# GpSimd's two-operand instructions of 512 columns in halves of 256, in a hybrid attention and RWKV block

## The chip, the cores and the metric

The kernel runs on one core of a Trainium2 chip. The metric is the device time of one execution in microseconds (us); the number that stands for a kernel is the median of its runs. Five engines work side by side, each through its own queue in order: TensorE (PE; its weight loads are PEld), VectorE (DVE), ScalarE (ACT), GpSimd (POOL) and SyncE (SP, which only issues DMAs here).

## What is computed

One layer of a residual block on 1024 frames of width 1024. The mixer has two groups of heads: A is sparse attention in which an indexer picks the 256 best keys of each frame, B is an RWKV-7 recurrence over 64-frame chunks. An MLP of width 4096 with squared ReLU follows. Cut to what matters:

```python
mod = silu(c) @ w_ada + b_ada                       # shift, scale, gate, twice
h = rms_norm(x, g_mix) * (1 + sc1) + sh1
proj = h @ w_in                                     # columns of group A, then of group B
o_a = dsa_attention(...)                            # index scores, top 256 keys, softmax
o_b = rwkv7_time_mix(token_shift(p_b, mu), ...)     # state * w + sa kk a + v k, per head
x = x + gt1 * (concat(o_a, o_b) @ w_out)
h = rms_norm(x, g_ffn) * (1 + sc2) + sh2
u = relu(h @ w_ff1)
x = x + gt2 * ((u * u) @ w_ff2)
```

## The kernel before

The 1024 frames are worked in two halves of 512 (`HALF`), features on the partitions and frames on the columns, so nearly every tile is 128 partitions x 512 columns.

**The large products.** `dense` (L391) makes one 128 x 512 product of `w_in`, `w_out`, `w_ff1` or `w_ff2`. Each operand is held as a rounded part and its remainder, and three matmuls take the place of one: hi x hi, hi x lo, lo x hi. For four blocks of weights at a time `load_w` (L378) fetches `wraw`, ACT rounds it to `whi` (L384), and POOL, or in the last stage DVE, subtracts: `wlo = wraw - whi` (L386). `LE = 'gggggggv'` says that POOL does it in all stages but the last, the MLP of the second half. `wlo` is 128 x 4 x 128, four buffers deep; the matmuls of `dense` read it one block of 128 columns at a time, in the order block 0, 1, 2, 3:

```python
mmul(ps[0:M], hi[:, k, 0:M], rh(K), start=(K == 0), stop=False)
mmul(ps[0:M], hi[:, k, 0:M], rl(K), start=False, stop=False)
mmul(ps[0:M], lo[:, k, 0:M], rh(K), start=False, stop=(K == nk - 1))
```

**The recurrence.** `rwkv_feat` (L486) prepares a pair of heads. POOL's part is `kp` (L523), `at` (L532), the second half of `KR` (L552), `wrec` (L558) and the two halves of `BKs` (L562, L563); DVE works between, with `rk` (L537), the first half of `KR` (L550) and `Bh` (L557). PE waits for `rk` with a product of its own. `rwkv_inv` inverts the chunk matrices with a long row of small DVE instructions, `rwkv_chain` runs the chunks, and `rwkv_out` normalises, with POOL's `On` (L718) and `ob` (L724). There are eight pairs of heads in all, four in each half. Which engine does such a step is set by `EM = 'gggggggggv'` through `EN`, whose result is GpSimd for `g`.

**The indexer.** `indexer` finds the 256th best score of each frame bit by bit, 31 bits: a count over the scores (`jk`, L911 and L913, on DVE; `jka`, L905, on ACT), then a few tiny DVE instructions (L926, L927, L902; L920, L928, L903) that set the next candidate. It runs beside the projections of the second half, and again beside the first MLP.

**The order of the work** is made by a scheduler that takes the instructions as the code gives them and sets them on the engines' queues by what it takes each to cost; a change of one engine's instructions can so move others.

Of the kernel before, what the change touches and what calls it, by code (L numbers as in the profile page):

```python
# [4 lines left out]
F32 = mybir.dt.float32  # L5
# [4 lines left out]
ALU = mybir.AluOpType  # L10
# [25 lines left out]
LE = 'gggggggv'  # L36
# [7 lines left out]
NL = 'gg'  # L44
# [3 lines left out]
EM = 'gggggggggv'  # L48
# [63 lines left out]
def body(tc, I, out, dbg=None):  # L112
    nc = tc.nc
    V, G, A, T = nc.vector, nc.gpsimd, nc.scalar, nc.tensor
# [5 lines left out]
    def mmul(out, lhsT, rhs, start=True, stop=True, **kw):  # L120
        r = T.matmul(out, lhsT, rhs, start=start, stop=stop, **kw)  # L121
        MM[0] = r
        if MK[0]:
            MARKS.append((MK[0], int(r.ins.name.split("-")[1])))
            MK[0] = None
        return r

    def EN(i):
        return V if EM[i] == "v" else G

    def mark(n):
        MK[0] = n
# [10 lines left out]
    def pst(tag):  # L143
        return pm.tile([128, 512], F32, name="ps_" + tag, tag=tag, bufs=BANKS[tag])
# [11 lines left out]
    def C(name, a=0, b=None):  # L156
        o, w = CC[name]
        t = con if o < NCF else conb
        o -= 0 if o < NCF else NCF
        return t[:, o + a:o + (w if b is None else b)]  # L160

    def P(name, a=0, b=None):
        o, w = PC[name]
        return prm[:, o + a:o + (w if b is None else b)]
# [21 lines left out]
    def sigmoid(out, x, bias=0.0):  # L186

        A.activation(out, x, AF.Tanh, scale=0.5, bias=bias)
        EN(8).tensor_scalar(out, out, 1.0, 0.5, ALU.add, ALU.mult)
# [104 lines left out]
    def h_tiles(hp=hp):  # L294
        hh = hp.tile([128, 8, HALF], F32R, name="hh", tag="hh", bufs=1)
        hl = hp.tile([128, 8, HALF], F32R, name="hl", tag="hl", bufs=1)
        return hh, hl
# [25 lines left out]
    def norm_last(hf, xn, xp, nb):  # L323
        mark('norm%d' % hf)
        hh, hl = h_tiles()
        for k in range(8):
            v = xp.tile([128, HALF], F32, name="nv", tag="nv", bufs=nb)
            V.tensor_scalar(v, xn[k], g1[:, k:k + 1], mod[:, k:k + 1], ALU.mult, ALU.add)
            A.copy(hh[:, k, :], v)
            (V if NL[hf] == "v" or k % 2 == 0 else G).tensor_tensor(hl[:, k, :], v, hh[:, k, :].bitcast(F32), ALU.subtract)  # L330
        return hh, hl

    def load_xT(hf, xp):
# [44 lines left out]
    def load_w(w, row0, col0, M):  # L378

        raw = wp.tile([128, 4, 128], F32, name="wraw", tag="wraw", bufs=WB[0])  # L380
        nc.sync.dma_start(raw[:, :, 0:M], w[row0:row0 + 512, col0:col0 + M].rearrange("(k p) n -> p k n", p=128))
        hi = wp.tile([128, 4, 128], F32R, name="whi", tag="whi", bufs=WB[1])
        lo = wp.tile([128, 4, 128], F32R, name="wlo", tag="wlo", bufs=WB[1])
        (A.copy if HE[GRP[0]] == "a" else V.tensor_copy)(hi[:, :, 0:M], raw[:, :, 0:M])  # L384
        GRP[1] ^= 1
        (V if LE[GRP[0]] == "v" or LE[GRP[0]] == "m" and GRP[1] else G).tensor_tensor(lo[:, :, 0:M], raw[:, :, 0:M], hi[:, :, 0:M].bitcast(F32), ALU.subtract)  # L386
        return hi, lo

    GRP = [0, 0]
# [63 lines left out]
    def spread(dst, i, j, sl):  # L453
        for h in range(2):
            nc.sync.dma_start(dst[h * 64:h * 64 + 64], rnd[i][2 * j + h:2 * j + h + 1, sl].to_broadcast([64, HALF]))
# [26 lines left out]
    def c3(x):  # L482
        return x.rearrange("p (c t) -> p c t", t=64)
# [4 lines left out]
    def rwkv_feat(hf, j, L4, rp, bp):  # L488

        mark('feat%d%d' % (hf, j))  # L490
        tw, xa, sg = L4
        sl = slice(hf * HALF, hf * HALF + HALF)

        def tmp(nm, tag=None, bufs=1):
            return rp.tile([128, HALF], F32, name=nm, tag=tag or nm, bufs=bufs)

        rT, kT = tmp("rT"), tmp("kT")
        v2 = rp.tile([128, 8, 64], F32, name="v2", tag="v2", bufs=1)
        nc.sync.dma_start(kT, rkvd[4 + j, :, sl])
        nc.sync.dma_start(rT, rkvd[j, :, sl])  # L500
        nc.sync.dma_start(v2, c3(rkvd[8 + j, :, sl]))
        gp = bp if j % 2 else rp
        KR, Lb = (gp.tile([128, 8, 2, 64], F32, name=n, tag=n, bufs=1) for n in ("KR", "Lb"))
        WC = gp.tile([128, 8], F32, name="WC", tag="WC", bufs=1)
        bvs = (bp if j % 3 else rp).tile([128, HALF], F32, name="bvs", tag=f"bvs{j % 3}", bufs=1)

        sig = rp.tile([128, 4, 128], F32, name="sig", tag="wincl", bufs=1)
        ps = pst("f")
        for tt in range(4):
            mmul(ps[:, tt * 128:tt * 128 + 128], tw[:, tt * 128:tt * 128 + 128], w2a[:, j * 128:j * 128 + 128])  # L510
        sigmoid(sig, ps.rearrange("p (a b) -> p a b", a=4))
        prn = tmp("prn", "aT")
        spread(prn, 0, j, sl)
        kap = tmp("kap")
        V.scalar_tensor_tensor(kap, kT, P("k_k", j, j + 1), prn, ALU.mult, ALU.mult)
        pa = pst("f")
        mmul(pa, a2w[:, j * 128:j * 128 + 128], xa)

        at = tmp("at", "aT")
        A.activation(at, pa, AF.Tanh, scale=0.5, bias=a0h[:, j:j + 1])  # L520
        kp = tmp("kp")
        A.activation(kp, at, AF.Identity, scale=kah[:, j:j + 1], bias=oka[:, j:j + 1])
        EN(0).tensor_tensor(kp, kp, kT, ALU.mult)  # L523
        b2 = at
        if FO == -1:
            G.tensor_scalar(at, at, 1.0, 0.5, ALU.add, ALU.mult)
            G.tensor_tensor(b2, kap, at, ALU.mult)
        elif FO == 0:
            V.scalar_tensor_tensor(b2, at, 1.0, kap, ALU.add, ALU.mult)
        elif FO == 1:  # L530
            A.activation(b2, at, AF.Identity, bias=1.0)
            G.tensor_tensor(b2, b2, kap, ALU.mult)  # L532
        else:
            G.tensor_scalar(b2, at, 1.0, 1.0, ALU.add, ALU.mult)
            G.tensor_tensor(b2, b2, kap, ALU.mult)
        rk = tmp("rk", "Bh")
        V.scalar_tensor_tensor(rk, rT, P("r_k", j, j + 1), kp, ALU.mult, ALU.mult)  # L537
        pb = pst("f")
        slow[hf, j] = mmul(pb, C("oblk"), rk)
        V.tensor_tensor(c3(bvs), c3(pb), v2, ALU.mult)  # L540
        pw = pst("f")
        for tt in range(4):
            mmul(pw[:, tt * 128:tt * 128 + 128], sig[:, tt, :], C("tri"))
        wi, wr = tmp("wincl"), tmp("wrec", bufs=2)
        A.activation(wi, pw, AF.Exp, scale=-EM05)
        A.activation(wr, pw, AF.Exp, scale=EM05)
        wi3 = c3(wi)
        V.tensor_copy(WC, wi3[:, :, 63])

        V.tensor_tensor(KR[:, :, 0, 1:64], c3(kap)[:, :, 1:64], wi3[:, :, 0:63], ALU.mult)  # L550
        V.tensor_copy(KR[:, :, 0, 0], c3(kap)[:, :, 0])
        EN(2).tensor_tensor(KR[:, :, 1, :], c3(rT), wi3, ALU.mult)  # L552
        Bh, Kh = tmp("Bh"), wr
        if FO == -1:
            V.tensor_tensor(Bh, b2, wr, ALU.mult)
        else:
            V.scalar_tensor_tensor(Bh, b2, 0.5, wr, ALU.mult, ALU.mult)  # L557
        EN(3).tensor_tensor(Kh, kp, wr, ALU.mult)  # L558
        gram(Bh, KR, Lb, "f")
        BKs = rp.tile([128, 8, 2, 64], F32, name="BKs", tag="BKs", bufs=1)  # L560
        wcb = WC.unsqueeze(2).to_broadcast([128, 8, 64])
        EN(4).tensor_tensor(BKs[:, :, 0, :], c3(Bh), wcb, ALU.mult)  # L562
        EN(5).tensor_tensor(BKs[:, :, 1, :], c3(Kh), wcb, ALU.mult)  # L563
        return dict(KR=KR, Lb=Lb, WC=WC, bvs=bvs, Kh=Kh, BKs=BKs, v2=v2)

    def gram(src, KR, dst, tag):
        for u in (0, 4):
            pz = pst(tag)
            for c in range(4):
                cc = u + c  # L570
                for h in range(2):
                    r = slice(h * 64, h * 64 + 64)
                    mmul(pz[r, c * 128:c * 128 + 128], src[r, cc * 64:cc * 64 + 64], flat(KR[r, cc, :, :]),
                         tile_position=(h * 64, h * 64))
            V.tensor_tensor(dst[:, u:u + 4, :, :].rearrange("p a b c -> p a (b c)"),
                            pz.rearrange("p (a b) -> p a b", a=4),
                            C("zmask").unsqueeze(1).to_broadcast([128, 4, 128]), ALU.mult)
# [738 lines left out]
```

## Time and profile before

| what | value |
|---|---|
| runs, median (lowest to highest of 3) | 1803.91 us (1803.64 to 1807.76) |
| profiled execution, its own time | 1806.86 us |
| its span, first to last instruction | 1805.0 us |
| PE busy | 1621.7 us, 90% |
| DVE busy | 1084.3 us, 60% |
| ACT busy | 870.9 us, 48% |
| POOL busy | 484.8 us, 27%, 423 instructions |
| mean granted clock of TensorE | 0.968 |

The profile is of one execution. An engine's busy share is a mean over the span; PE's matmuls overlap, so its busy time is no measure of how full it is. POOL has no work in the last 375 us: its last `wlo` starts at 1429.1 us. An instruction's time in the trace reaches from its start to its end and holds what it waited for after its start.

### The profile page before, as it was taken

What the parts mean: (1) busy time and instruction counts of PE and PEld (TensorE: products, weight loads), DVE (VectorE), ACT (ScalarE), POOL (GpSimd) and SP (SyncE); (2) the same over time, 40 slices, a digit from 0 to 9 for tenths busy, and PEclk for the clock granted to TensorE, in tenths of its full rate; (3) what the DMA queues carried; (4) which work ended last, traced back from release to release, by engine and by line L of the source; (5) the groups of instructions that cost most, each with busy time, mean ns of one, the idle gap of its engine ahead of it and who ended that gap; (6) DMA issues with size and microseconds to landing.
All of it is one profiled execution on the core that took longest, in us unless ns stands there. A gap on an engine that the chain in (4) does not pass through costs nothing. (4 is left out here: it accounts for less than half of the span.)

```text
span 1805.0 us, 26789 instructions
## 1 busy us (share of the span) xinstructions
PE 1621.7 (90%) x9380; PEld 1210.2 (67%) x9380; DVE 1084.3 (60%) x2701; ACT 870.9 (48%) x1792; POOL 484.8 (27%) x423
## 2 busy tenths in 40 slices
PE   6896888998779887998968888999999999999998
PEld 3674655666555565665647666777886788888887
DVE  4787677649987666846999648773213333333333
ACT  3323454545546544544855773775335252525251
POOL 2445333343340133332123343012444300000000
PEclk9998999999989999999978999999999999999999
DMA  9785225334343452212112234233432343333332
GB/s 309 248 298 181 84 69 176 110 91 135 99 113 104 151 159 83 80 51 70 48 41 70 70 94 129 79 86 116 124 95 75 100 128 94 99 94 98 96 94 75
DMA packets 264013, 203.86 MB, mean 113 GB/s; under 512 B 17300, under 2 KB 218004, under 8 KB 263879
## 3 DMA queue, kind: packets, MB, share of 16 engines
q1 hardware_dynamic: 253122, 182.90, 34.1%
q10 hardware_dynamic: 10628, 19.24, 2.8%
q8 instruction: 74, 1.21, 0.3%
q14 instruction: 61, 0.49, 0.1%
q0 software_dynamic: 128, 0.01, 0.0%
HBM read 173.32 MB, written 28.78 MB: 112 GB/s over the span
## 5 line engine op out<-in xcount | busy, mean ns | idle before, releaser
L386 POOL TENSOR_TENSOR wlo<-wraw,whi 128x512 fp32r<-128x512 f32 x256 | 345.1, 1352 | 741.4 <-ACT whi L384 632.0
L384 ACT CAST whi<-wraw 128x512 fp32r<-128x512 f32 x384 | 235.8, 617 | 418.4 <-PE ps_mm L121 384.9
L121 PE MATMUL ps_mm<-hh,whi 128*128 128x512 f32 (+1 forms) x1024 | 415.3, 407 | 20.8 <-DVE shy L428 6.7
L121 PE MATMUL ps_mm<-hh,wlo 128*128 128x512 f32 (+1 forms) x1024 | 415.5, 406 | 5.3 <-POOL wlo L386 5.1
L121 PE MATMUL ps_mm<-hl,whi 128*128 128x512 f32 (+1 forms) x1024 | 416.1, 407 | 3.5 <-DVE hl L374 2.0
L121 PEld LDWEIGHTS ps_mm<-hh,whi 128*128 128x128 f32 (+1 forms) x1024 | 194.2, 190 | 68.4 <-DVE shy L428 8.4
L121 PEld LDWEIGHTS ps_mm<-hh,wlo 128*128 128x128 f32 (+1 forms) x1024 | 194.4, 190 | 50.3 <-POOL wlo L386 10.0
L121 PEld LDWEIGHTS ps_mm<-hl,whi 128*128 128x128 f32 (+1 forms) x1024 | 194.6, 190 | 45.9 <-issue 5.1
L121 PE MATMUL ps_mm<-uh,whi 128*128 128x512 f32 x512 | 206.9, 405 | 18.7 <-ACT whi L384 5.4
L121 PE MATMUL ps_mm<-ul,whi 128*128 128x512 f32 x512 | 206.6, 404 | 5.8 <-DVE ul L1108 5.8
L121 PE MATMUL ps_mm<-uh,wlo 128*128 128x512 f32 x512 | 206.3, 403 | 2.0 <-POOL wlo L386 1.9
L386 DVE TENSOR_TENSOR wlo<-wraw,whi 128x512 fp32r<-128x512 f32 x128 | 88.3, 690 | 130.1 <-ACT whi L384 130.1
L905 ACT ACTIVATE jka<-sc,canda 128x1024 bf16<-128x1024 f32 (+1 forms) x93 | 90.2, 970 | 86.8 <-DVE canda L903 59.4
L121 PEld LDWEIGHTS ps_mm<-uh,whi 128*128 128x128 f32 x512 | 98.9, 193 | 46.1 <-ACT whi L384 9.4
L121 PEld LDWEIGHTS ps_mm<-ul,whi 128*128 128x128 f32 x512 | 98.7, 193 | 29.9 <-DVE ul L1108 8.0
L121 PEld LDWEIGHTS ps_mm<-uh,wlo 128*128 128x128 f32 x512 | 98.9, 193 | 26.6 <-POOL wlo L386 4.0
L1114 DVE SCALAR_TENSOR_TENSOR xT<-ps_mm,mod,xT 128x512 f32<-128x512 f32 x64 | 47.9, 749 | 111.6 <-PE ps_mm L121 111.5
L1108 DVE TENSOR_TENSOR ul<-ur,uh 128x512 fp32r<-128x512 f32 x64 | 44.2, 691 | 80.0 <-ACT uh L1107 80.0
L1013 DVE CUSTOM_DVE_ANT_0 L<-ps_f,mk 128x512 f32<-128x512 f32 (+3 forms) x96 | 51.8, 554 | 34.3 <-PE ps_f L121 16.9
L695 ACT COPY Ub<-ps_c 64x64 f32<-64x64 f32 x128 | 26.3, 206 | 74.1 <-DVE UV L693 65.3
L1019 ACT ACTIVATE L<-L,m 128x128 f32<-128x128 f32 (+7 forms) x64 | 49.6, 775 | 18.6 <-DVE m L1016 13.8
L1032 ACT COPY PT<-ps_c 128x512 f32<-128x512 f32 (+3 forms) x96 | 42.6, 479 | 31.0 <-PE ps_c L1031 29.3
(329 smaller groups left out, 2623.1 us busy)
## 6 DMA issues: line engine op xcount, KB each, us to landing
wraw<-in_w_ff_dram SPq DMA_DIRECT2D x256, 256.0 KB
wraw<-in_w_in_dram SPq DMA_DIRECT2D x92, 256.0 KB
mraw<-in_w_ada_dram SPq DMA_DIRECT2D x64, 256.0 KB
mraw<-in_w_ada_dram SPq DMA_DIRECT2D x16, 512.0 KB
wraw<-in_w_out_dram SPq DMA_DIRECT2D x32, 256.0 KB
rkvd<-shy ACTq DMA_DIRECT2D x24, 256.0 KB
xin<-in_x_dram SPq DMA_DIRECT2D x8, 512.0 KB
rt<-rnd SPq DMA_DIRECT2D x32, 128.0 KB
```

What stands on the lines that cost most here:

```text
L121: r = T.matmul(out, lhsT, rhs, start=start, stop=stop, **kw)
L384: (A.copy if HE[GRP[0]] == "a" else V.tensor_copy)(hi[:, :, 0:M], raw[:, :, 0:M])
L386: (V if LE[GRP[0]] == "v" or LE[GRP[0]] == "m" and GRP[1] else G).tensor_tensor(lo[:, :, 0:M], raw[:, :, 0:M], hi[:, :, 0:M].bitcast(F32), ...
L695: (V.tensor_copy if CE[2] == "v" else A.copy)(Ub[h * 64:h * 64 + 64, h, :], pu[u, h * 64:h * 64 + 64])
L905: A.activation(jka[:, 0:width(b)], sc[b], AF.Sign, scale=-1.0, bias=0.0 if bit == 31 else canda.bitcast(F32)[:, i:i + 1], accum_out=ca[:, ...
L1013: V.tensor_tensor_reduce(L[:, c0:c0 + n], ps[:, 0:n], masks[b][:, c0:c0 + n], 1.0, -3e38, ALU.add, ALU.max, m2[:, pc:pc + 1])
L1019: A.activation(L[:, 0:W], L[:, 0:W], AF.Exp, bias=m2[:, 2:3], accum_out=m2[:, 3:4])
L1032: (A.copy if ((pc + h) % 2 if PTE == 0 else h if PTE == 1 else PTE == 2) else V.tensor_copy)(pT[:, c0:c0 + n], px[:, 0:n])
L1108: V.tensor_tensor(b, r, a.bitcast(F32), ALU.subtract)
L1114: V.scalar_tensor_tensor(xT[:, d, :], ps, mod[:, 40 + d:41 + d], xT[:, d, :], ALU.mult, ALU.add)
```

## The change

A class `InHalves` stands where `G` (GpSimd) stood: in `EN`, in `norm_last`, in `load_w` and in `rwkv_feat`. Its `tensor_tensor` issues two instructions, one on the first half of the second axis and one on the other; its `tensor_scalar` is GpSimd's as it was. The second axis of `wlo` has four blocks of 128 columns, so a half is two blocks; of the others it has 512 columns or 8 chunks. The narrow `wlo` of 4 x 72 columns is cut to 2 x 72 as well. Nothing else is changed: what is computed, which engine does it, buffers and DMAs are the same. Split are 256 `wlo`, 8 `hl`, and eight each of `kp`, `at`, `KR`, `wrec`, `On`, `ob` and the two `BKs`: 328 instructions become 656.

```diff
+    class InHalves:
+
+        tensor_scalar = G.tensor_scalar
+
+        @staticmethod
+        def tensor_tensor(o, a, b, op):
+            n = o.shape[1] // 2
+            for c in (slice(0, n), slice(n, 2 * n)):
+                G.tensor_tensor(o[:, c], a[:, c], b[:, c], op)
+
     def EN(i):
-        return V if EM[i] == "v" else G
+        return V if EM[i] == "v" else InHalves
...
-            (V if NL[hf] == "v" or k % 2 == 0 else G).tensor_tensor(hl[:, k, :], v, hh[:, k, :].bitcast(F32), ALU.subtract)
+            (V if NL[hf] == "v" or k % 2 == 0 else InHalves).tensor_tensor(hl[:, k, :], v, hh[:, k, :].bitcast(F32), ALU.subtract)
...
-        (V if LE[GRP[0]] == "v" or LE[GRP[0]] == "m" and GRP[1] else G).tensor_tensor(lo[:, :, 0:M], raw[:, :, 0:M], hi[:, :, 0:M].bitcast(F32), ALU.subtract)
+        (V if LE[GRP[0]] == "v" or LE[GRP[0]] == "m" and GRP[1] else InHalves).tensor_tensor(lo[:, :, 0:M], raw[:, :, 0:M], hi[:, :, 0:M].bitcast(F32), ALU.subtract)
...
-            G.tensor_tensor(b2, b2, kap, ALU.mult)
+            InHalves.tensor_tensor(b2, b2, kap, ALU.mult)
```

The order of the instructions shows it at three places. The first is POOL's queue at the first pair of heads (`rwkv_feat`); before:

```order
L523 TENSOR_TENSOR kp<-kp,kT 128x512
L532 TENSOR_TENSOR at<-at,kap 128x512
L386 TENSOR_TENSOR wlo<-wraw,whi 128x512 x3
L552 TENSOR_TENSOR KR<-rT,wincl 128x8x64
L558 TENSOR_TENSOR wrec<-kp,wrec 128x512
```

and now, where every split instruction is at L136:

```order
L136 TENSOR_TENSOR kp<-kp,kT 128x256 x2
L136 TENSOR_TENSOR at<-at,kap 128x256 x2
L136 TENSOR_TENSOR wlo<-wraw,whi 128x256 x6
L136 TENSOR_TENSOR KR<-rT,wincl 128x4x64 x2
L136 TENSOR_TENSOR wrec<-kp,wrec 128x256 x2
```

The steps stand in the same order, each as two.

The second is PE's queue in the projections of the first half, with what a matmul waits for; `wlo` is the weights' remainder and Pool_49 POOL's semaphore. Before:

```order
L121 MATMUL ps_mm<-hh,wlo 128x512 [waits Pool_49]
L121 MATMUL ps_mm<-hh,whi 128x512
L121 MATMUL ps_mm<-hl,whi 128x512
L121 MATMUL ps_mm<-hh,wlo 128x512
L121 MATMUL ps_mm<-hh,whi 128x512
L121 MATMUL ps_mm<-hl,whi 128x512
L121 MATMUL ps_mm<-hh,wlo 128x512
```

and now:

```order
L121 MATMUL ps_mm<-hh,wlo 128x512 [waits Pool_49]
L121 MATMUL ps_mm<-hh,whi 128x512
L121 MATMUL ps_mm<-hl,whi 128x512
L121 MATMUL ps_mm<-hh,wlo 128x512
L121 MATMUL ps_mm<-hh,whi 128x512
L121 MATMUL ps_mm<-hl,whi 128x512
L121 MATMUL ps_mm<-hh,wlo 128x512 [waits Pool_49]
```

The first matmul with `wlo` waits for the first half alone, and the one on block 2, six matmuls later, for the second.

The third is ACT's queue where the first search of the indexer begins (`rl` are index scores, `jka` its counts on ACT); before:

```order
L867 ACTIVATE rl<-ps_f 128x384
L867 ACTIVATE rl<-ps_f 128x512
L384 CAST whi<-wraw 128x512
L905 ACTIVATE jka,ca<-sc_3837 128x512
L419 DMA rkvd<-shy 128x512
L384 CAST whi<-wraw 128x512
L905 ACTIVATE jka,ca<-sc_3837,canda 128x512
```

and now:

```order
L394 CAST whi<-wraw 128x512
L877 ACTIVATE rl<-ps_f 128x384
L877 ACTIVATE rl<-ps_f 128x512
L429 DMA rkvd<-shy 128x512
L915 ACTIVATE jka,ca<-sc_3925 128x512
L394 CAST whi<-wraw 128x512
L915 ACTIVATE jka,ca<-sc_3925,canda 128x512
```

One rounding of weights stands two score tiles earlier, and a DMA ahead of the first count instead of behind it. Such shifts lie between PE's rows 988 and 2203 of some 6050, from the last pair of heads of the first half to the start of the second indexer (in the trace of before, from 400 to some 845 us); ahead of them and behind them PE's order is the same.

## Rows read from the trace of the kernel before

**Rows 1.** Busy time by stretch: PE, PEld, DVE, ACT, POOL, granted clock, DMA share, GB/s.
```profile
0.00:1100.00 1100.00, 931.98 (x5951) 660.48 (x5952) 797.79 (x2161) 561.17 (x1252) 378.06 (x341) 0.95 0.39 121
1100.00:1805.00 705.00, 689.73 (x3431) 549.75 (x3429) 286.56 (x541) 309.75 (x540) 106.74 (x82) 1.00 0.34 100
...
900.00:1000.00 100.00, 81.05 (x293) 60.12 (x294) 96.57 (x270) 51.69 (x95) 31.01 (x22) 0.83 0.19 56
```

**Rows 2.** POOL's groups by shape (busy us, mean ns, idle before); last, L386's minimum/median/maximum.
```profile
L386 POOL TENSOR_TENSOR wlo<-wraw,whi 128x512 fp32r<-128x512 f32 x252 | 341.9, 1360 | 726.8 <-ACT whi L384 624.4 <-PE ps_mm L121 39.7 <-DMA kr<-khd 16.0
L386 POOL TENSOR_TENSOR wlo<-wraw,whi 128x288 fp32r<-128x288 f32 x4 | 3.2, 801 | 14.6 <-ACT whi L384 7.6 <-ACT On L703 4.5 <-DMA prn<-rnd 2.5
...
L386 POOL TENSOR_TENSOR wlo<-wraw,whi x256: 791/1289/2042, 39.6 to 1429.1; 128x512 fp32r<-128x512 f32 x126, 128x288 fp32r<-128x288 f32 x2
```

**Rows 3.** Timeline of DVE, then POOL, at 150 us (start, us, instruction).
```profile
150.44 1.64 DVE L281 SCALAR_TENSOR_TENSOR macc<-mraw,cs,macc 128x512 f32<-128x512 f32 x1
152.00 1.75 DVE L537 SCALAR_TENSOR_TENSOR rk<-rT,prm,kp 128x512 f32<-128x512 f32 x1
...
150.26 1.28 POOL L523 TENSOR_TENSOR kp<-kp,kT 128x512 f32<-128x512 f32 x1 [4.20 <-ACT kp L522]
151.50 1.71 POOL L532 TENSOR_TENSOR at<-at,kap 128x512 f32<-128x512 f32 x1
```

**Rows 4.** Timeline of DVE, then POOL, at 930 us, in the second indexer.
```profile
930.49 1.01 DVE L911 TENSOR_SCALAR_CACHE_REDUCE jk<-top,cand 128x768 bf16<-128x768 bf16 x1
...
931.54 0.37 DVE L926 TENSOR_SCALAR acc<-cv 128x2 int32<-128x2 f32 x1
931.95 1.19 DVE L927 TENSOR_TENSOR pre<-pre,acc 128x2 int32<-128x2 int32 x1
...
930.61 2.50 POOL L386 TENSOR_TENSOR wlo<-wraw,whi 128x512 fp32r<-128x512 f32 x2 [6.25 <-ACT whi L384]
```

**Rows 5.** DVE's groups by shape (busy us, mean ns, idle before).
```profile
L926 DVE TENSOR_SCALAR acc<-cv 128x2 int32<-128x2 f32 x31 | 15.1, 488 | 0.5
L926 DVE TENSOR_SCALAR acc<-cv 128x1 int32<-128x1 f32 x31 | 4.7, 152 | 0.6
L928 DVE TENSOR_TENSOR prea<-prea,acca 128x1 int32<-128x1 int32 x31 | 14.7, 474 | 0.2
L281 DVE SCALAR_TENSOR_TENSOR macc<-mraw,cs,macc 128x512 f32<-128x512 f32 x56 | 51.7, 923 | 2.3 <-DMA mraw<-in_w_ada_dram 0.8
L1114 DVE SCALAR_TENSOR_TENSOR xT<-ps_mm,mod,xT 128x512 f32<-128x512 f32 x64 | 47.9, 749 | 111.6 <-PE ps_mm L121 111.5
L550 DVE TENSOR_TENSOR KR<-kap,wincl 128x504 f32<-128x504 f32 x8 | 11.2, 1406 | 0.1
L754 DVE TENSOR_TENSOR rt<-rt 128x512 f32<-128x512 f32 x8 | 5.5, 686 | 0.1
L537 DVE SCALAR_TENSOR_TENSOR rk<-rT,prm,kp 128x512 f32<-128x512 f32 x8 | 10.1, 1259 | 2.7 <-POOL kp L523 2.7
```

**Rows 6.** PE's waits by releaser: us in total, times, longest.
```profile
PE ps_f L121 <- DVE rk L537: 14.3, 6, 6.8
PE ps_f L121 <- DVE acca L920: 7.9, 1, 7.9
PE ps_mm L121 <- POOL wlo L386: 7.0, 11, 1.1
PE ps_mm L121 <- DVE acca L920: 6.2, 5, 1.7
PE ps_c L721 <- POOL On L718: 2.7, 2, 2.1
```

**Rows 7.** Timeline of PE, POOL and ACT at 1033 us.
```profile
1034.59 0.50 PE L121 MATMUL ps_mm<-hh,wlo 128*128 128x512 f32 x1 [0.62 <-POOL wlo L386]
...
1033.26 1.27 POOL L386 TENSOR_TENSOR wlo<-wraw,whi 128x512 fp32r<-128x512 f32 x1 [2.44 <-ACT whi L384]
...
1032.56 0.62 ACT L384 CAST whi<-wraw 128x512 fp32r<-128x512 f32 x1
```

## The prediction

> **What bounds the kernel now.** I read the busy time by stretch first. Up to 1100 us the stages are mixed: PE is busy for 932 of 1100 us, DVE for 798. Behind that PE is busy for 690 of 705 us and little can be won; POOL has work there until 1429 us, but PE hardly waits for it [rows 1]. PE's queue sets the pace throughout, and what this change can move is PE's waiting in the first 1100 us. The second indexer is the tightest place of DVE: from 900 to 1000 us it is busy for 96.6 us, PE for 81, and PE's granted clock is 0.83 there [rows 1].
>
> PE's waits by releaser come next. For POOL itself PE waits little: 7.0 us for `wlo`, 2.7 us for `On`. It waits more for DVE: 14.3 us for `rk`, 7.9 and 6.2 us put down to the indexer's counts [rows 6]. The timelines show what POOL has to do with that. At 150.44 us DVE issues a sum (`macc`) and is done only at 152.08, as POOL's `kp` ends at 151.54; then `rk` stands from 152.00 to 153.75 until POOL's `at` has ended at 153.21; and POOL's `at` itself takes 1.71 us because it stood behind the DVE sum [rows 3]. At 931.95 us a DVE instruction on two columns takes 1.19 us beside POOL's `wlo`, while the count of 768 columns just ahead of it ran its 1.01 us beside the same POOL work undisturbed [rows 4]. So POOL's two-operand instructions and part of DVE's shut each other out, one whole instruction at a time, and between two POOL instructions one waiting DVE instruction gets through: at 931.54 DVE goes after the first of POOL's pair, and the next DVE instruction waits for the second [rows 4].
>
> What that costs DVE is read from its groups, mean against the mean of the like group that meets no POOL work [rows 5]: the count's step L926 (488 - 152) x 31 = 10.4 us, L928 (474 - 152) x 31 = 10.0, `macc` (923 - 749) x 56 = 9.7, `KR` (1406 - 686) x 8 = 5.8, `rk` (1259 - 749) x 8 = 4.1: 40.0 us in five groups.
>
> **The price of a half.** No POOL row has 256 columns; the nearest is the narrow `wlo` with 288: 801 ns against 1360 for 512 [rows 2]. The line through both means gives 2.50 ns a column and 82 ns fixed, so 722 ns for a half and 1444 for the pair, 84 more than before. Through the median 1289 in place of the mean, 2.18 ns a column and 174 fixed: 732 and 1463, 174 more. I take 0.13 us a pair, with both as ends. 328 pairs make 43 us more on POOL, which is busy for 485 of 1805 us: hidden, as long as nobody waits for the second half. If the cover went, it would be the 14 pairs of the third term that pay. The Trainium skill's GPSIMD Engine Reference (section Performance versus the Vector engine) puts a two-input instruction at about 2.6 cycles an element at 1.2 GHz; an estimate from it is 555 ns for 256 columns, and with the median's remainder of 180 ns each the third term would be 2.5 us in place of 1.8. No row here shows it at 256.
>
> **The terms.**
> First, `wlo` comes earlier: its first two blocks land after 0.72 us in place of 1.29, and PE needs the other two only six matmuls later. Eleven PE waits of together 7.0 us end with it [rows 6]; 0.57 us off each would be 6.3 us at most. But six of them, 0.6 us each, lie between 1030 and 1050 us and look like the one shown, where ACT rounds `whi` with no idle time in front of it [rows 7]: PE would reach the next `whi` sooner and wait there. Of the other five I take 2 us: **-2**, between -6.3 and 0.
>
> Second, blocked DVE instructions. Where POOL's pair is `wlo`, made ahead of time, and the DVE instruction let in after the first half is the last that needs POOL's way, the second half runs beside undisturbed DVE work and half of the block is gone. Where another such DVE instruction follows at once, the second half blocks that one, and the sum stays. In the indexer three tiny ones follow each other ahead of an undisturbed count, so one in three: 20.4 x 1/3 x 1/2 = 3.4 us, and 4 with the like of the groups not shown. For `macc`, back to back, nothing; for `rk` and `KR` nothing, since there the POOL instruction is itself on the way to the same result, and two jobs behind one door take their sum in either order. **-4**, between -10 (half of all 40 us, and half of that on the path, as 28.4 us of PE's waits stand behind these chains [rows 6]) and 0.
>
> Third, POOL's results that PE waits for come later: six waits for `rk` with two split steps ahead of them (`kp`, `at`) and two for `On` [rows 6], 14 pairs x 0.13 = 1.8: **+2**. If a DVE instruction of 512 columns (0.75 us [rows 5]) slips between the halves each time, 14 x 0.75 = 10.5 us more.
>
> The added semaphore waits on PE I cost at nothing: they are for the second half, and the six matmuls ahead of it cover more than its 0.72 us. DVE and ACT get no instruction more, SP's DMAs are the same, and what stands behind a POOL instruction in POOL's queue is moved by the 0.13 us alone. The scheduler's shifts between 400 and 845 us have no row that prices them; I take 0, with 1 us on either end.
>
> The sum is -4 us. The profiled execution took 1806.9 us, 3 us above the median of the runs (1803.9); against its own time the sum gives 1802.9, against the median **1800**.
>
> **The rivals.** A change within 0.3% (5.4 us) is about what a measurement of this kernel cannot tell from none.
>
> *Faster, DVE is freed.* If most blocked DVE instructions stand alone, every block halves: term two is -10, and 1803.9 - 2 - 10 + 2 gives **1794**. For it: PE's waits behind DVE are the largest of the mixed stages [rows 6], and DVE fills the second indexer, where the clock is low too [rows 1]. Against it: at 931 us it was the very next DVE instruction that the second POOL instruction held [rows 4]. Chance 0.37.
>
> *No change, as many blocks as before.* In the runs of small DVE instructions, each half shuts out one. The second term is then 0, and the port's time grows by 0.13 us for each of some 20 blocks in L926 and L928 (20.4 us at nearly 1 us each): +3. 1803.9 - 2 + 3 + 2 = **1807**. The Trainium skill's page SBUF — State Buffer (section Who interferes with whom) has it that issue order, not the shape of the operation, decides who is blocked; by that rule a smaller shape wins nothing as such. Rows 4 bear it out as far as one DVE instruction goes through between two of POOL's. Chance 0.13. It also stands for the change not doing what it says: if POOL's second half takes the way before the waiting DVE instruction, two halves block like one whole, and the time is near 1804.
>
> *Slower, POOL's own chain is cut in two.* Each of the 14 pairs that PE waits for lets a DVE instruction in between its halves, one that used to wait until the whole was done: `macc` at 150.44 would now go in the middle of `kp`, and `rk` waits for `kp` [rows 3]. That is 10.5 us: 1803.9 - 2 + 10.5 + 2 = **1814**. It decides from some seven such pairs up (7 x 0.75 = 5.3), if the second term is nothing. Against it: the same interposed work need not be done later, so on `rk`'s way much comes back. Chance 0.22.
>
> **How the numbers follow.** The forecast of 1800 has 0.28. It and the rival near 1807 lie within 0.3%: 0.41. Faster by more, 0.37; slower by more, 0.22. The range reaches from 1803.9 - 6.3 - 10, and 1 for the order, 1786.6, rounded to 1786, to the slower rival's 1814 and 1 for the order, 1815. The outer tenth on either side is left for the scheduler's shifts and for PE's clock, whose low stretches neither bound holds.
>
> **What would show it.** Right: POOL's halves near 0.72 us and 656 of them; the six `wlo` waits at 1030 us gone and waits for `whi` in their place; L926 and L928 at means some 15% lower, with the other tiny instructions of the search a little longer; `rk` and `KR` as long as before, give or take the order. Wrong: if `rk`, `KR` and L926 all come down by half of their excess, DVE was freed; if PE's waits for `rk` and `On` grow by half a us each, the chain was cut; if the time moves between 400 and 845 us alone, it was the order.

## The result, and the profile after

The changed kernel takes **1789.09 us** (median of 5 runs, 1783.01 to 1792.60) beside 1805.34 us (5 runs, 1803.64 to 1807.97) for the kernel before: a ratio of 0.99, 95% interval 0.9876 to 0.9923. It is faster by 1%. The forecast of 1800 us, no change that can be told, was 11 us too long; the range of 1786 to 1815 holds the time, and of the rivals the one that frees DVE (1794) came nearest.

The profiled execution took 1783.31 us, at the low end of the runs, with a span of 1781.5 us (1805.0 before). The page's first part:

```profile
PE 1613.9 (91%) x9380; PEld 1208.7 (68%) x9380; DVE 1060.6 (60%) x2701; ACT 871.5 (49%) x1792; POOL 557.7 (31%) x751
```

DVE does the same 2701 instructions in 23.7 us less; POOL needs 72.9 us more. PE's busy time falls by 7.8 us and the span by 23.5, so two thirds of the gain are PE's idle time (183.3 us before, 167.6 after). The other third is PE's own work: the same 9380 matmuls, at a mean granted clock of 0.971 beside 0.968.

POOL's groups by shape (busy us, mean ns, idle before), against [rows 2]:

```profile
L136 POOL TENSOR_TENSOR wlo<-wraw,whi 128x256 fp32r<-128x256 f32 x504 | 396.5, 810 | 643.8 <-ACT whi L394 582.3 <-DMA kr<-khd 15.9 <-PE ps_mm L121 10.8
L136 POOL TENSOR_TENSOR wlo<-wraw,whi 128x144 fp32r<-128x144 f32 x8 | 4.1, 527 | 14.3 <-ACT whi L394 7.5 <-ACT On L713 4.3 <-DMA prn<-rnd 2.4
```

A half has a mean of 810 ns with what it waited for; undisturbed, a pair takes 1.44 us (below), 0.72 a half, as the prediction had it.

DVE's groups by shape, against [rows 5] (lines are 10 higher; L936, L938, L291, L560 and L547 are L926, L928, L281, L550 and L537):

```profile
L936 DVE TENSOR_SCALAR acc<-cv 128x2 int32<-128x2 f32 x31 | 10.0, 322 | 0.5
L938 DVE TENSOR_TENSOR prea<-prea,acca 128x1 int32<-128x1 int32 x31 | 7.7, 247 | 0.3
L291 DVE SCALAR_TENSOR_TENSOR macc<-mraw,cs,macc 128x512 f32<-128x512 f32 x56 | 50.3, 899 | 3.0 <-DMA mraw<-in_w_ada_dram 1.4
L560 DVE TENSOR_TENSOR KR<-kap,wincl 128x504 f32<-128x504 f32 x8 | 7.3, 918 | 0.1
L547 DVE SCALAR_TENSOR_TENSOR rk<-rT,prm,kp 128x512 f32<-128x512 f32 x8 | 8.8, 1097 | 3.0 <-POOL kp L136 3.0
L937 DVE TENSOR_TENSOR pre<-pre,acc 128x2 int32<-128x2 int32 x31 | 10.4, 335 | 0.8
```

By the working of the prediction the excess of the five groups goes from 40.0 us to (322 - 152) x 31 = 5.3, (247 - 152) x 31 = 2.9, (899 - 749) x 56 = 8.4, (918 - 686) x 8 = 1.9 and (1097 - 749) x 8 = 2.8, together 21.3: close to half. But part of that only moved. L937, the step behind L936, grew from 295 to 335 ns, and so did the step behind L938, which is L903 before and L913 now:

```profile
L903 DVE SCALAR_TENSOR_TENSOR canda<-prea,xma 128x1 int32<-128x1 int32 x31 | 7.8, 253 | 0.2
```

```profile
L913 DVE SCALAR_TENSOR_TENSOR canda<-prea,xma 128x1 int32<-128x1 int32 x31 | 9.8, 317 | 0.2
```

There a second half blocks the next instruction. All groups of the search's small steps (`acc`, `pre`, `prea`, `cand`, `canda`) went from 80.4 to 76.1 us together: of the 12.1 us that L936 and L938 lost, the steps behind them took 7.8 back. So DVE's 23.7 us are 4.3 from these steps, 6.6 from `macc`, `KR` and `rk`, and 12.8 spread over its other instructions, no group of which lost more than 2.6.

Both cases stand in the timelines. At the first pair of heads, DVE's row and then POOL's, against [rows 3]:

```profile
145.87 1.89 DVE L291 SCALAR_TENSOR_TENSOR macc<-mraw,cs,macc 128x512 f32<-128x512 f32 x2
148.38 1.19 DVE L547 SCALAR_TENSOR_TENSOR rk<-rT,prm,kp 128x512 f32<-128x512 f32 x1 [0.62 <-POOL kp L136]
...
146.46 1.88 POOL L136 TENSOR_TENSOR kp<-kp,kT 128x256 f32<-128x256 f32 x2 [2.38 <-ACT kp L532]
148.30 1.86 POOL L136 TENSOR_TENSOR at<-at,kap 128x256 f32<-128x256 f32 x2
```

`kp` takes 1.88 us in place of 1.28, because a DVE sum (the second `macc`) goes between its halves; but `rk` then stands only behind the first half of `at`, and is done 3.11 us after `kp` began (148.38 + 1.19 - 146.46) in place of 3.49. In the second indexer, against [rows 4]:

```profile
913.77 0.53 DVE L936 TENSOR_SCALAR acc<-cv 128x2 int32<-128x2 f32 x1
914.33 0.65 DVE L937 TENSOR_TENSOR pre<-pre,acc 128x2 int32<-128x2 int32 x1
915.00 0.65 DVE L912 SCALAR_TENSOR_TENSOR cand<-pre,xmh 128x2 int32<-128x2 int32 x1
915.69 0.88 DVE L921 TENSOR_SCALAR_CACHE_REDUCE jk<-top,cand 128x640 bf16<-128x640 bf16 x1
...
912.84 2.80 POOL L136 TENSOR_TENSOR wlo<-wraw,whi 128x256 fp32r<-128x256 f32 x4 [5.56 <-ACT whi L394]
```

Two `wlo` follow each other, and three tiny DVE instructions pay for three of the four halves: 1.92 us from 913.77 to the next count, about the 1.83 us of before, from 931.54 [rows 4] to this count:

```profile
933.37 0.88 DVE L911 TENSOR_SCALAR_CACHE_REDUCE jk<-top,cand 128x640 bf16<-128x640 bf16 x1
```

Here nothing was won. One DVE instruction goes through between every two of POOL's.

PE's waits by releaser, against [rows 6]:

```profile
PE ps_f L121 <- DVE rk L547: 15.7, 7, 5.3
PE ps_f L121 <- DVE acca L930: 8.4, 1, 8.4
PE ps_mm L121 <- ACT whi L394: 7.0, 7, 2.5
PE ps_c L731 <- POOL On L136: 5.7, 2, 3.5
...
PE ps_mm L121 <- DVE acca L930: 5.0, 3, 2.5
...
PE ps_mm L121 <- POOL wlo L136: 0.5, 1, 0.5
```

The waits for `wlo` are gone (7.0 to 0.5 us). All of PE's waits that a DVE instruction ended add up to 119.9 us before and 106.9 now, those that POOL ended to 13.0 and 9.1. What came in their place in the second indexer, against [rows 7], is a wait for ACT, half as long; PE, POOL and ACT at 1014 us:

```profile
1017.30 0.50 PE L121 MATMUL ps_mm<-hh,whi 128*128 128x512 f32 x1 [0.30 <-ACT whi L394]
...
1013.65 1.44 POOL L136 TENSOR_TENSOR wlo<-wraw,whi 128x256 fp32r<-128x256 f32 x2 [2.29 <-ACT whi L394]
...
1016.64 0.61 ACT L394 CAST whi<-wraw 128x512 fp32r<-128x512 f32 x1
```

Where along the program the time was won is read from three lines that occur at fixed places: `rk` once for each pair of heads, the counts `jka` of both searches, and the output projection's `xT`. From the instructions of one line (count, minimum/median/maximum ns, first to last start in us); before:

```profile
L537 DVE SCALAR_TENSOR_TENSOR rk<-rT,prm,kp x8: 740/1244/1807, 152.0 to 702.8; 128x512 f32<-128x512 f32 x8
L905 ACT ACTIVATE jka<-sc,canda x93: 708/1043/1159, 439.2 to 1073.4; 128x512 bf16<-128x512 f32 x31, 128x896 bf16<-128x896 f32 x31, 128x1024 bf16<-128x1024 f32 x31
L1061 DVE SCALAR_TENSOR_TENSOR xT<-ps_mm,mod,xT x16: 709/751/752, 739.6 to 1339.7; 128x512 f32<-128x512 f32 x16
```

and after:

```profile
L547 DVE SCALAR_TENSOR_TENSOR rk<-rT,prm,kp x8: 739/1194/1254, 148.4 to 678.6; 128x512 f32<-128x512 f32 x8
L915 ACT ACTIVATE jka<-sc,canda x93: 704/1043/1157, 429.6 to 1052.8; 128x512 bf16<-128x512 f32 x31, 128x896 bf16<-128x896 f32 x31, 128x1024 bf16<-128x1024 f32 x31
L1071 DVE SCALAR_TENSOR_TENSOR xT<-ps_mm,mod,xT x16: 741/750/751, 728.0 to 1316.3; 128x512 f32<-128x512 f32 x16
```

The lead is 3.6 us at 152 us, 9.6 at the first search, 24.2 at the last `rk`, only 11.6 at the first `xT`, 20.6 at the end of the second search and 23.4 at the last `xT`. (These are two single executions, and that of the changed kernel is one of its two fastest; the medians lie 16 us apart.) It grows all along the mixed stages; between `rk` and `xT`, inside the stretch whose order the scheduler shifted, 12.6 us are given back. The longest `rk` falls from 1807 to 1254 ns: the whole of `at` in front of it has become a half.

### The profile page after: what moved, and what is told of

Read it like the earlier page. It is cut to its first block, busy times and chain, and to the rows that moved or that the text cites. A ratio compares the mean times of both kernels' runs of the same rounds, so it can differ in the third digit from the quotient of the medians.

```text
span 1781.5 us, 27231 instructions
## 1 busy us (share of the span) xinstructions
PE 1613.9 (91%) x9380; PEld 1208.7 (68%) x9380; DVE 1060.6 (60%) x2701; ACT 871.5 (49%) x1792; POOL 557.7 (31%) x751
## 5 line engine op out<-in xcount | busy, mean ns | idle before, releaser
L136 POOL TENSOR_TENSOR wlo<-wraw,whi 128x256 fp32r<-128x256 f32 x512 | 400.6, 805 | 658.1 <-ACT whi L394 589.9
```

What stands on the lines that cost most here:

```text
L136: G.tensor_tensor(o[:, c], a[:, c], b[:, c], op)
```

## The experiments

Theory A: DVE is let in after half a block, that is the gain. Theory B: the scheduler's shifts are the gain. Theory C: PE gets the first two blocks of `wlo` earlier, that is the gain. Which instructions are in halves decides the scheduler's order, and it can be chosen: with `KR` and `On` in halves PE's order is that of the changed kernel, without them that of before. Each ratio is to runs of the kernel before on the same chip, 5 rounds.

**The order alone, and the halves alone.**

```diff
-        return V if EM[i] == "v" else InHalves
+        return V if EM[i] == "v" else InHalves if i in (2, 6) else G
```

with `G` at the three other places (order_only), and

```diff
+        return V if EM[i] == "v" else G if i in (2, 6) else InHalves
```

with the rest as in the changed kernel (halves_old_order).

> Only KR and On, 16 of the 328 instructions, are in halves; PE's order is row for row that of the changed kernel. Theory A (DVE's blocks beside POOL are halved, that is the gain): within 4 us of the kernel before. Theory B (the scheduler's shifts between 400 and 845 us are the gain): 10 to 16 us faster. Theory C (PE gets the first half of wlo earlier): within 4 us of before, as A.

Measured: **1.0014** (0.9993 to 1.0035). The order is no gain; theory B falls.

> 312 of the 328 instructions are in halves, KR and On are whole; PE's order is row for row that of the kernel before. Theory A: 12 to 18 us faster than before, like the changed kernel, with some 110 us of DVE groups' excess in blocks of near 0.45 us. Theory B: within 4 us of before. Theory C: 12 to 18 us faster.

Measured: **0.9854** (0.9831 to 0.9878), and a second time, on another chip, 0.9856 (0.9838 to 0.9874):

> halves_old_order a second time, on another chip. If keeping the old order (with KR and On whole) is worth something over the changed kernel (0.99 and 0.9913 in two tries), it lies at 0.983 to 0.988 again; if its first result was that chip's, at 0.989 to 0.992.

That is 26 us faster than before, more than theories A and C were given, and better than the changed kernel, which had 0.99 and, tried again beside other kernels, 0.9913 (0.9892 to 0.9934):

> The changed kernel again, beside the others on one chip. If the scheduler's shifts cost 3 to 9 us (order_only and all_but_wlo against before and wlo_only), it lies 3 to 9 us above halves_old_order's 0.9854 of before, at 0.987 to 0.991, and no faster than wlo_only; if they cost nothing, at 0.984 to 0.987.

What the shifted stretch costs shows in the same two lines; order_only:

```profile
L547 DVE SCALAR_TENSOR_TENSOR rk<-rT,prm,kp x8: 733/1238/1805, 153.9 to 699.7; 128x512 f32<-128x512 f32 x8
...
L1071 DVE SCALAR_TENSOR_TENSOR xT<-ps_mm,mod,xT x16: 742/751/753, 748.6 to 1349.6; 128x512 f32<-128x512 f32 x16
```

and halves_old_order:

```profile
L547 DVE SCALAR_TENSOR_TENSOR rk<-rT,prm,kp x8: 747/1196/1254, 148.4 to 685.4; 128x512 f32<-128x512 f32 x8
...
L1071 DVE SCALAR_TENSOR_TENSOR xT<-ps_mm,mod,xT x16: 739/750/751, 721.2 to 1315.0; 128x512 f32<-128x512 f32 x16
```

From the last `rk` to the first `xT` the old order takes 36.8 us (before) and 35.8, the new one 49.4 (after) and 48.9. Part of it is only shifted, as the new order reaches that `rk` earlier. From the first `rk` to the first `xT` it is 587.6 us before and 594.7 with order_only, 572.8 with halves_old_order and 579.6 after: some 7 us for the new order with `KR` and `On` in halves, in both pairs. Over the whole kernel that is resolved with the other halves (0.99 and 0.9913 against 0.9854 and 0.9856) and not without them (1.0014). Order and those 16 instructions were not separated.

**`wlo` alone, and all but `wlo`.** `InHalves` in `load_w` only, order of before (wlo_only); and in all places but `load_w`, order of the changed kernel (all_but_wlo).

> Only the 256 wlo are in halves, PE's order is that of before. Theory A: wlo is the blocker of some two thirds of the blocked DVE instructions, so 8 to 12 us faster. Theory B: no change within 4 us. Theory C: the whole gain, 14 to 18 us faster, and the waits of PE for wlo go from 7 us to under 2 us.

Measured: **0.9886** (0.9861 to 0.9912), 1791.58 us beside 1810.41. `wlo` alone brings the bulk. That exceeds what theory A was given, and does not tell A from C.

> 72 instructions (hl, kp, at, KR, wrec, BKs, On, ob) are in halves, wlo is whole; PE's order is that of the changed kernel. Theory A: 3 to 6 us faster than before (a third of the blocks). Theory B: 10 to 16 us faster. Theory C: no change within 4 us.

Measured: **0.9997** (0.9976 to 1.0017). The other steps, in the new order, bring nothing: theory A's 3 to 6 us did not come. A gain of theirs and the cost of the order can cancel here.

**`wlo` with the last half first.** Now PE's first matmul with `wlo` waits for both halves again, DVE is let in as before, and the order of PE, DVE, ACT and SP is row for row that of the kernel before:

```diff
-            for c in (slice(0, n), slice(n, 2 * n)):
+            for c in (slice(n, 2 * n), slice(0, n)):
```

> Only wlo in halves, issued last half first, so that PE's first matmul with wlo waits for both, as before; the order of PE, DVE, ACT and SP is row for row that of the kernel before. Theory A (DVE is let in after half a block): 14 to 22 us faster than before, like wlo_only (which measured 0.9886 of before). Theory C (PE gets wlo earlier): within 4 us of before, and PE's waits for wlo back at 6 us or more.

Measured: **0.9904** (0.9873 to 0.9934). PE's waits for `wlo` are back, and the gain stays; theory C falls. PE's waits, then one DVE group and DVE's busy time:

```profile
PE ps_mm L121 <- POOL wlo L136: 7.0, 11, 1.2
```

```profile
L936 DVE TENSOR_SCALAR acc<-cv 128x2 int32<-128x2 f32 x31 | 10.0, 322 | 0.5
```

```profile
PE 1616.9 (91%) x9380; PEld 1211.2 (68%) x9380; DVE 1066.8 (60%) x2701; ACT 870.6 (49%) x1792; POOL 542.3 (30%) x679
```

L936 comes down to the same 322 ns, DVE's work is 17.5 us shorter than before, PE's waits that DVE ended add up to 109.0 us (119.9 before), and so little hangs on the first blocks that wlo_only and wlo_back cannot be told apart.

**The size of the parts.** `wlo` in three blocks and one, in four, and in eight parts of 64 columns:

```diff
-            n = o.shape[1] // 2
-            for c in (slice(0, n), slice(n, 2 * n)):
+            n = 3 * (o.shape[1] // 4)
+            for c in (slice(0, n), slice(n, o.shape[1])):
```

> Only wlo, in instructions of three blocks and one (384 and 128 columns). Theory A: the long part still blocks DVE for some 0.65 us, so a bit over half of the gain of wlo_only, 8 to 14 us faster than before. Theory C: the first part lands 0.3 us earlier than the whole, under half of the gain, 2 to 6 us.

Measured: **0.99** (0.9879 to 0.9921), 18 us faster than before: more than theory A was given for it, and not told from wlo_only. DVE's work does stand where theory A puts it, between the two: 1071.1 us, beside 1067.5 with wlo_only and 1084.3 before.

```diff
-            n = o.shape[1] // 2
-            for c in (slice(0, n), slice(n, 2 * n)):
+            n = o.shape[1] // 4
+            for c in (slice(n * i, n * i + n) for i in range(4)):
```

> Only wlo, in four instructions of one block each (128 columns). Theory A: blocks of DVE of some 0.25 us, 3 to 8 us faster than wlo_only, if the fixed price of an instruction (0.17 to 0.2 us, three more of them for each of 256 wlo, 40 to 50 us more on POOL than wlo_only per hundred) stays hidden; where that price decides, as slow as wlo_only or slower. Theory C: no faster than wlo_only by more than 2 us, since its waits for wlo are already under 1 us.

Measured: **0.9802** (0.9778 to 0.9825), 1772.88 us beside 1808.20: nearly twice the gain of the halves' 0.9886, though POOL has 100 us more to do. The `wlo` group and the first part of the page:

```profile
L136 POOL TENSOR_TENSOR wlo<-wraw,whi 128x128 fp32r<-128x128 f32 x1008 | 499.4, 527 | 570.2 <-ACT whi L394 491.7 <-DMA kr<-khd 15.6 <-DMA vd<-vs 14.9
```

```profile
PE 1610.8 (91%) x9380; PEld 1206.9 (68%) x9380; DVE 1042.9 (59%) x2701; ACT 869.7 (49%) x1792; POOL 646.5 (36%) x1191
```

DVE's work is 41.4 us shorter than before, more than all the 40.0 us that the prediction counted in its five groups. In eight parts:

```diff
+            n = o.shape[2] // 2
+            for k in range(4):
+                for c in (slice(0, n), slice(n, 2 * n)):
+                    G.tensor_tensor(o[:, k, c], a[:, k, c], b[:, k, c], op)
```

> Only wlo, in eight instructions of 64 columns; PE's order is that of before. A 128-column part took 0.53 us, a 256-column part 0.81, so about 0.39 us a part and 3.1 us a wlo by the line through them. Theory A alone: DVE's blocks shrink again, at 0.974 to 0.980 of before. If the fixed price decides now (some 800 us of work for POOL, blocks of DVE no smaller than the fixed part, wlo late for PE): 0.980 to 0.990, slower than wlo_quarters' 0.9802, with PE's waits for wlo growing past 5 us.

Measured: **0.9913** (0.9887 to 0.9939), more than half of the quarters' gain given back. The `wlo` group, the first part, and two of PE's waits:

```profile
L137 POOL TENSOR_TENSOR wlo<-wraw,whi 128x64 fp32r<-128x64 f32 x2016 | 702.9, 386 | 424.2 <-ACT whi L395 377.1 <-DMA vd<-vs 14.9 <-ACT PT L1043 8.7
```

```profile
PE 1636.3 (91%) x9380; PEld 1219.3 (68%) x9380; DVE 1028.8 (57%) x2701; ACT 870.5 (48%) x1792; POOL 849.4 (47%) x2215
```

```profile
PE ps_f L121 <- DVE rk L548: 18.3, 7, 5.6
...
PE ps_mm L121 <- POOL wlo L137: 6.8, 13, 1.1
```

DVE's work is shorter still, so it is not DVE that loses here. POOL, busy for 849 us, comes late: PE's waits that POOL ended add up to 21.0 us, beside 6.8 with quarters. At the first pair of heads ACT has its part of `kp` done at 152.16 us, and POOL, with a `wlo` in eight parts in front, begins its own at 155.12; ACT, then POOL:

```profile
151.35 0.81 ACT L533 ACTIVATE kp<-at,oka,kah 128x512 f32<-128x512 f32 x1
...
150.33 4.24 POOL L137 TENSOR_TENSOR wlo<-wraw,whi 128x64 fp32r<-128x64 f32 x8
154.54 0.62 POOL L200 TENSOR_SCALAR sig<-sig 128x512 f32<-128x512 f32 x1
155.12 1.26 POOL L534 TENSOR_TENSOR kp<-kp,kT 128x512 f32<-128x512 f32 x1
```

But PE's idle time is only 6.9 us longer than with quarters (167.9 and 161.0). The other 25.5 of the 32.4 us between the two profiled executions are PE's own work, at a granted clock of 0.960 beside 0.974. And this execution was the slowest of the kernel's runs (1805.9 us). So POOL's lateness is seen, and how much of the loss it makes stays open.

**The best of them.** `wlo` in quarters, the other steps in halves, `KR` and `On` whole, so that the order is that of before (best_mix); and the other steps in quarters too (all_quarters).

```diff
+    class InQuarters:
+        @staticmethod
+        def tensor_tensor(o, a, b, op):
+            for k in range(4):
+                G.tensor_tensor(o[:, k:k + 1], a[:, k:k + 1], b[:, k:k + 1], op)
```

> wlo in quarters, the other split steps in halves, KR and On whole, PE's order that of before. By halves_old_order against wlo_only (0.9854 against 0.9886) the other steps give some 5 us in the old order: 0.975 to 0.979 of before, 2 to 9 us faster than wlo_quarters. If they are worth nothing: 0.979 to 0.982.

Measured: **0.9752** (0.9731 to 0.9774), 1765.08 us beside 1810.37: 45 us faster than the kernel before, and faster than both kernels of this study.

> wlo and the other split steps in quarters, KR and On whole, PE's order that of before. Theory A: as best_mix or up to 4 us faster. If the fixed price weighs on the steps that the recurrence waits for (kp, at, wrec, BKs, some 0.35 us more for each step than in halves): 2 to 8 us slower than best_mix.

Measured: 0.9786 (0.9768 to 0.9804), 1771.52 us, 6 us slower than best_mix; the intervals still touch. Quarters of the other steps bring nothing more. That the fixed price of an instruction weighs there, in steps that the recurrence waits for, would explain it and was not shown.

## Why the prediction was right and wrong

The mechanism was read rightly, and the sum was too small in one term. That the measured time lies in the range all the same is in part luck: the scheduler's shifts, put at nothing, cost time and hid some of the gain.

- **What bounds the kernel** held. POOL and DVE shut each other out an instruction at a time, one waiting DVE instruction goes between two of POOL's, and the time was won in the mixed stages; behind the second search the lead no longer grows by more than 3 us.
- **The price of a half** held: 1.44 us a pair undisturbed, the lower end of the 1444 to 1463 ns forecast. (That no POOL row had 256 columns is so for two operands alone; a COPY of 32x256 took 421 ns.) With what the halves wait for, POOL's work grew by 72.9 us, 0.22 a pair in place of 0.13; it stayed hidden.
- **First term**, -2 for the earlier `wlo`: the waits for `wlo` went, and in the second search shorter waits for `whi` came, as said. wlo_only against wlo_back gives 0.0018, some 3 us: near the term, but inside both intervals, so it is not shown.
- **Second term**, -4 for blocked DVE instructions, -10 at most: this is the step that failed. wlo_back, in which PE gets nothing earlier and no order moves, measured 1 - 0.9904 of 1808 us, that is -17 us (-12 to -23), with 256 of the 328 instructions. In the search the working was right: the small steps lost 4.3 us together, with wlo_back as in the changed kernel (76.1 us in both), where 3.4 were forecast. Too small was all the rest. `macc`, `KR` and `rk`, put at nothing, lost 6.6 us. The groups that were not listed, put at 0.6 us, lost 12.8; and with quarters DVE lost 41.4 us, more than the 40.0 that were taken for the whole excess. On the path, 28.4 us of PE's waits were counted behind the listed DVE groups, where PE's waits behind all of DVE add up to 119.9; these fell by 13.0 (10.9 with wlo_back). Another 7.8 us (4.8 with wlo_back) went from PE's own work, at a granted clock of 0.971 (0.969) beside 0.968, and that had no term.
- **Third term**, +2 for POOL's own chain: at the first pair `rk`'s way became shorter (3.11 in place of 3.49 us), not longer. PE's waits for `rk` and `On` grew by 1.4 and 3.0 us, twice the term. That for `rk` lies anywhere between 6.8 (wlo_only) and 25.3 us (best_mix) and tells nothing. That for `On` is 5.2 to 5.8 us in the profiles with `On` in halves and 2.7 to 4.8 in those with it whole; the former all have the new order too, so the halves are not shown to be the cause.
- **The scheduler's shifts**, 0 with 1 us on either side, were mis-sized too: with `KR` and `On` in halves they cost 8 to 11 us beside the other halves (0.0044 to 0.0059 of 1808 us). Without that the range would have missed: halves_old_order's 0.9854 of 1803.9 is 1778.
- **Of the rivals**, "DVE is freed" was right in its sign, and its price (-10) too small. The sign that was named for it, half of the excess gone from `rk`, `KR` and L926 alike, came near: a third (510 to 348 ns), two thirds (720 to 232) and half (336 to 170). "As many blocks as before" is seen in the search, where most of the blocking moved on; but that a smaller shape wins nothing as such is not borne out, since wlo_back changes little else and won 17 us. "POOL's own chain is cut in two" happens just as it was described (`macc` goes into the middle of `kp`) and costs nothing there, since `rk` gets back at `at` what it lost at `kp`.

The runs of the changed kernel lie between 1783 and 1793 us; the two lowest have a granted clock of 0.971, the two highest 0.963 and 0.965. The faster kernels have the higher clock too: the median is 0.964 to 0.965 in the runs of the kernel before, 0.970 with halves_old_order, 0.974 with best_mix. Whether PE's shorter waits raise it was not tried, nor what sets it back in some executions and not in others.

## What to carry to other kernels

Where two engines shut each other out for the length of an instruction, the one whose work is made ahead of time should hold the door briefly: cut its instructions, and go on cutting while the kernel gets faster (here 128 columns won, and 64 lost, with the cut engine's other results late). Judge by the waiting engine's whole busy time, and not by a few groups or one timeline: the two steps of the search that lost most here handed two thirds of it to the instructions behind them, and half of the whole came from many small groups. DVE's busy time fell by 17.5 us with wlo_back, 41.4 with quarters and 46.4 with best_mix, and the kernel's time by 17, 36 and 45; with eighths the two part. Look at what a scheduler does with the change, and undo that part by itself: here two of ten steps moved the order, and leaving them whole added about half of the gain again.

## What the runs showed of the hardware

The price of GpSimd's subtraction is nearly a line: 1.27 to 1.29 us for 512 columns, 0.72 for 256, and with what it waited for 0.53 for 128 and 0.39 for 64, so that a fixed part of roughly 0.2 us stays at any size. That a queue of two GpSimd instructions lets one VectorE instruction through between them was seen before the change; that it does so between four of them, one each time, was not expected; nor that cutting them further still paid with GpSimd busy for 37% of the span (best_mix), and no longer as much at 47% (wlo_eighths). VectorE's instructions on a single column, 0.15 us of work, were blocked just as those of 512.
